# A hybrid decoder step on one core: projection steps and attention units put into one interleaved list, and the input norm done in small parts

## The chip, the cores and the metric

The kernel runs on one core of one Trainium2 chip. The metric is device time in microseconds (us); a run's time is that of one execution. The profile is one further execution, recorded by the hardware.

## The reference, cut to what matters

One layer of a decoder: an RMS norm, one input projection `w_in` to queries, keys, values and a pooling input u, stick-breaking attention (8 heads of 64) beside a multi-scale pooling mixer, an output projection, and a gated FFN with a short convolution. There are 2048 prompt rows of width 1024 behind 16 meta rows, and 8 decode rows with a paged cache. All is fp32.

```python
def rmsnorm(x, g):
    xf = x.astype(jnp.float32)
    r = lax.rsqrt(jnp.mean(xf * xf, axis=-1, keepdims=True) + EPS)
    return (xf * r * g.astype(jnp.float32)).astype(x.dtype)

h = rmsnorm(xp, norm_mix_g)
q, k, v, u = project_mix(h, w_in)
...
z = jnp.einsum('bqhd,bkhd->bhqk', q, k) * ATTN_SCALE + sb_bias[None, :, None, None]
valid = k_pos[None, :] < q_pos[:, None]
neg = jnp.where(valid, -jax.nn.softplus(z), 0.0)
suffix = lax.cumsum(neg, axis=3, reverse=True) - neg
a = jnp.where(valid, jnp.exp(jax.nn.log_sigmoid(z) + suffix), 0.0)
o = jnp.einsum('bhqk,bkhd->bqhd', a, v)
...
xp = xp + jnp.concatenate([o_attn, o_pool], axis=-1) @ w_out
```

## The kernel before

Every large product is made from fp32 numbers split in a rounded high part and a rest (`split`, L152: ScalarE copies, VectorE subtracts), in three matmuls a term (`mm3`, L156). A scheduler orders the instructions of each engine ahead of time: the order in which the program is written is a priority, an instruction takes its place when its simulated inputs and its buffer are ready, and each engine, the SP queue of the DMAs among them, then runs its own list strictly in order.

The mixer works on four *groups* of 128 projected columns (q, k, v and u of one pair of heads) and four *chunks* of 512 prompt rows. `prep_chunk` (L200) makes one chunk ready: for each of four tiles of 128 rows it loads x, squares it on ScalarE with a row sum (`rstd_of`, L130), runs twelve tiny VectorE operations for the reciprocal root (L138 to L149) and multiplies by root and norm weight (`norm_rows`, L192, with the weight broadcast over all partitions in `gmix`). Then, for each of eight blocks of 128 features, TensorE transposes the four tiles into one PSUM tile `tpx` (L209), it is split into `hk`, and `hk` is also stored to `hs_s` in DRAM (L212), from where groups 1 to 3 load it again (`load_h`, L215). `prep_small` (L222) does the same for the 24 decode and meta rows.

`group_steps(g)` (L351) lists 16 steps, four chunks by q, k, v, u. A step loads and splits weights where a group needs new ones (`load_w`, L231, for q and k together, then for v and u, with the few rows in `few_rows`, L240), and calls `project` (L303): 24 matmuls of 512 columns into `psm`, a copy to SBUF, and stores to DRAM scratch (`q_s`, `k_s`) and to the outputs, keys and values through four more transposes (`put_tok`, L294). The step of u makes window sums, and the one of chunk 1 also folds the pooling weights into the output weights (`fold_pool`, L334: two loads `wt` and a matmul on each, L346). There are 11 buffers for `hk`, so in groups 1 to 3 the last step of a chunk loads three blocks of the next chunk ahead and the other five behind its own matmuls.

`attention(hp)` (L383) works on one pair of heads in 45 *units*: a block of 128 queries (or the 16 meta rows, `bi` = -1) by a chunk of up to 512 keys, the chunks from the last key to the first. `chain` (L430) makes the scores into `z` (L450), two sigmoids on ScalarE (L451, L452), a running product on VectorE (the scan, L458) and a product that VectorE and GpSimd take in turn (L463). `weigh` (L472) follows three units later (`LAG`): it transposes the weights into `tt` (L493), copies them to SBUF on ScalarE or VectorE (L486) and multiplies by V into `po` (L508). Queries and keys come back from DRAM scratch and are split (`load_q` L387, `load_k` L399) when the first unit of a query block asks for them.

The order around the change is written out as: all 16 steps of group 0, then `attention(0)` with the steps of group 1 spread evenly between its units, `attention(1)` with group 2, `attention(2)` with group 3, then the output weights, then `attention(3)`, in which each finished block of 128 rows is followed, one block later, by its output projection and second norm (`out_tile`, L573). Decode attention and the FFN come after that, from 1175 us on.

Of the kernel before, what the change touches and what calls it, by code (L numbers as in the profile page):

```python
# [18 lines left out]
P = 128  # L19
D = 1024  # L20
# [19 lines left out]
LAG = 3  # L40
BEB, OMB, ATB = 5, 3, 4
# [17 lines left out]
def hymba_kernel(  # L59
# [70 lines left out]
    def rstd_of(pool, xt, n, sq=None):  # L130
# [6 lines left out]
        ms = pool.tile([P, 1], F32, name="ms")  # L137
        nc.vector.tensor_scalar(out=ms[:n, :], in0=ss[:n, :], scalar1=1.0 / D, scalar2=EPS, op0=ALU.mult, op1=ALU.add)  # L138
        r = pool.tile([P, 1], F32, name="rr")
        t = pool.tile([P, 1], F32, name="rt")  # L140
# [4 lines left out]
        for _ in range(3):  # L145
            nc.vector.scalar_tensor_tensor(out=t[:n, :], in0=r[:n, :], scalar=r[:n, 0:1], in1=ms[:n, :],
                                           op0=ALU.mult, op1=ALU.mult)
# [34 lines left out]
    gmix = [pb.tile([P, CW], F32, name=f"gmix{q}", tag="raw", bufs=RWB) for q in range(2)]  # L182

    def load_x(i):
        xt = pb.tile([P, 2, CW + 1], F32, name="xt", tag="om", bufs=OMB).rearrange("p a n -> p (a n)")[:, 0:D]
        x_rows(xt, i)
        if i == 1:
            for q in range(2):
                nc.sync.dma_start(out=gmix[q], in_=norm_mix_g[q * CW:(q + 1) * CW].partition_broadcast(P))
        return xt  # L190

    def norm_rows(xt, n, r):  # L192
        xn = pb.tile([P, 2, CW], F32, name="xn", tag="be", bufs=BEB).rearrange("p a n -> p (a n)")
        for q in range(2):
            cs = slice(q * CW, (q + 1) * CW)
            nc.vector.scalar_tensor_tensor(out=xn[:n, cs], in0=xt[:n, cs], scalar=r, in1=gmix[q][:n, :],
                                           op0=ALU.mult, op1=ALU.mult)
        return xn

    def prep_chunk(ch):  # L200
        xns = []
        for a in range(4):
            xt = load_x(1 + 4 * ch + a)
            xns.append(norm_rows(xt, P, rstd_of(pb, xt, P, sq=("at", ATB))[:, 0:1]))
        hk = []
        for c in range(NK):
            tp = tt_tile("tpx")
            for a in range(4):
                nc.tensor.transpose(tp[:, a, :], xns[a][:, c * P:(c + 1) * P], ident)  # L209
            hk.append(pa.tile([P, 2, CW], F32R, name="hk", bufs=HKB))  # L210
            split(hk[c][:, 0, :], hk[c][:, 1, :], tp.rearrange("p a n -> p (a n)"))
            nc.sync.dma_start(out=hs_s[ch][c], in_=f32(hk[c]))  # L212
        return hk
# [872 lines left out]
```

## Time and profile before

| what | us |
|---|---|
| median of 3 runs | 2874.93 |
| lowest and highest | 2872.41, 2880.97 |
| the profiled execution's own time | 2876.12 |
| its span, first to last instruction | 2874.3 |

In the profile, PE is TensorE's matmuls, PEld its weight loads, which overlap them, DVE is VectorE, ACT ScalarE, POOL GpSimd, SP the queue that issues nearly all DMAs. L12 is line 12 of the kernel before. Matmuls are pipelined, so busy TensorE can be TensorE that waits for its operands between two of them; what it does in a stretch is better read from how many matmuls it finishes there. PEclk is the mean clock granted to TensorE, 1.00 being 2.4 GHz; its lower level is 1.2 GHz. The view of waits and the idle time in brackets name the instruction that ended the wait last.

### The profile page before, as it was taken

The numbers are of one execution on the slowest core, as the hardware profiler recorded it, in microseconds if no ns is written. First come the engines' busy times: TensorE is split into PE (matmuls) and PEld (weight loads), VectorE is DVE, ScalarE is ACT, GpSimd is POOL, SyncE is SP. The second block draws the span as 40 slices with busy tenths as digits, with TensorE's granted clock in tenths as the row PEclk, the third lists the DMA queues.
The fourth block names the chain that finished last, engine by engine and source line by source line (L and its number), as shares of the span: only waits on it lengthen the run. The fifth ranks groups of instructions, "written<-read, shape, count | busy, mean of one in ns | idle before, by whom it ended". The sixth has DMA issues, their size and how long they took to land.

```text
span 2874.3 us, 39685 instructions
## 1 busy us (share of the span) xinstructions
PE 2724.3 (95%) x14622; PEld 2106.8 (73%) x14622; DVE 1826.1 (64%) x3101; ACT 1041.3 (36%) x1801; POOL 825.5 (29%) x995
## 2 busy tenths in 40 slices
PE   5899999999998999799999998999999999999998
PEld 4677777777776777577777776777777767777766
DVE  6556787687787778579876766677764451124433
ACT  3345665665665356322322222222222230012111
POOL 0023243333233222044554454445543200000000
PEclk9899999999998999889999999999999999999999
DMA  6674344333425332466566465546655385656552
GB/s 210 241 256 147 112 132 169 114 119 119 143 67 173 113 100 91 154 201 205 195 246 216 169 232 198 179 158 227 212 183 198 129 279 172 189 181 209 161 202 88
DMA packets 319223, 495.10 MB, mean 172 GB/s; under 512 B 24111, under 2 KB 227127, under 8 KB 302629
## 3 DMA queue, kind: packets, MB, share of 16 engines
q1 hardware_dynamic: 300597, 358.35, 38.4%
q0 software_dynamic: 18432, 134.23, 12.8%
q8 instruction: 115, 1.88, 0.3%
q14 instruction: 79, 0.65, 0.1%
HBM read 391.27 MB, written 101.64 MB: 171 GB/s over the span
## 4 chain that ended last, share of the span: by engine, by line
PE 60%; DVE 8%; DMA 4%; issue 3%; ACT 1%; POOL 0%; SPq 0%; ACTq 0%; DVEq 0%; POOLq 0%
PE psu L159 10%; PE psu L160 9%; PE psu L161 9%; PE psd L159 5%; PE psd L161 5%; PE psd L160 5%; PE dav L804 2%; PE po L508 2%; DVE kvd L736 1%; PE z L450 1%; PE pso L161 1%; PE pso L159 1%; PE pso L160 1%; PE tt L493 1%; DVE om L458 1%
## 5 line engine op out<-in xcount | busy, mean ns | idle before, releaser
L159 PE MATMUL psu<-h2c,uwh 128*128 128x512 f32 x1408 | 557.1, 396 | 0.7 <-ACT h2c L153 0.7
L160 PE MATMUL psu<-h2c,uwh 128*128 128x512 f32 x1408 | 553.2, 393 | 0.0
L161 PE MATMUL psu<-h2c,uwl 128*128 128x512 f32 x1408 | 552.9, 393 | 0.0
L458 DVE TENSOR_TENSOR_SCAN om<-om,zero 128x513 f32<-128x513 f32 (+5 forms) x360 | 381.5, 1066 | 103.4 <-ACT om L451 60.3
L884 DVE SCALAR_TENSOR_TENSOR cv<-psu,par,cv 128x511 f32<-128x511 f32 (+1 forms) x352 | 261.2, 742 | 130.3 <-ACT cv L881 129.3
L463 POOL TENSOR_TENSOR be<-be,om 128x512 f32<-128x512 f32 (+3 forms) x176 | 182.4, 1036 | 550.0 <-DVE om L458 310.5
L159 PEld LDWEIGHTS psu<-h2c,uwh 128*128 128x128 f32 x1408 | 266.5, 189 | 82.8 <-issue 15.8
L160 PEld LDWEIGHTS psu<-h2c,uwh 128*128 128x128 f32 x1408 | 266.4, 189 | 63.7 <-issue 9.7
L161 PEld LDWEIGHTS psu<-h2c,uwl 128*128 128x128 f32 x1408 | 266.2, 189 | 63.6 <-issue 8.3
L451 ACT ACTIVATE om<-z,nbias 128x512 f32<-128x512 f32 (+5 forms) x360 | 213.2, 594 | 214.0 <-PE z L450 125.4
L895 POOL TENSOR_TENSOR cv<-cv,cv 128x512 f32<-128x512 f32 x88 | 195.4, 2221 | 267.6 <-DVE cv L889 215.9
L1053 DVE TENSOR_TENSOR xt<-psd,xt 128x512 f32<-128x512 f32 x64 | 44.1, 690 | 293.6 <-PE psd L161 287.1
L881 ACT ACTIVATE cv<-psu,par 128x512 f32<-128x512 f32 x176 | 136.4, 776 | 252.1 <-PE psu L161 241.2
L154 DVE TENSOR_TENSOR uwl<-uwr,uwh 128x1024 fp32r<-128x1024 f32 x94 | 128.1, 1364 | 152.5 <-ACT uwh L153 150.2
L159 PE MATMUL psm<-hk,wh 128*128 128x512 f32 x512 | 207.2, 410 | 6.3 <-ACT wh L153 4.2
L452 ACT ACTIVATE be<-z,bias 128x512 f32<-128x512 f32 (+5 forms) x360 | 211.1, 589 | 1.0 <-PE tpx L209 0.9
L160 PE MATMUL psm<-hk,wh 128*128 128x512 f32 x512 | 209.0, 408 | 0.0
L161 PE MATMUL psm<-hk,wl 128*128 128x512 f32 x512 | 206.4, 403 | 0.0
L161 PE MATMUL psd<-wd,al 128*128 128x512 f32 x512 | 200.9, 393 | 0.0
L159 PE MATMUL psd<-wd,ah 128*128 128x512 f32 x512 | 200.8, 396 | 0.0
L160 PE MATMUL psd<-wd,ah 128*128 128x512 f32 x512 | 200.4, 392 | 0.0
L153 ACT CAST uwh<-uwr 128x1024 fp32r<-128x1024 f32 x94 | 99.0, 1056 | 270.3 <-PE psu L160 258.2
(226 smaller groups left out, 4892.1 us busy)
## 6 DMA issues: line engine op xcount, KB each, us to landing
hk<-hs_s SPq DMA_DIRECT2D x96, 512.0 KB
uwr<-in_w_up_dram SPq DMA_DIRECT2D x88, 512.0 KB
act_s<-sg SPq DMA_DIRECT2D x88, 256.0 KB
ar<-act_s SPq DMA_DIRECT2D x32, 704.0 KB
raw<-in_w_up_dram SPq DMA_DIRECT2D x40, 512.0 KB
xt<-in_x_prompt_dram SPq DMA_DIRECT2D x32, 512.0 KB
hs_s<-hk SPq DMA_DIRECT2D x32, 512.0 KB
uwr<-in_w_down_dram SPq DMA_DIRECT2D x22, 512.0 KB
```

The source lines that it names most:

```text
L153: nc.scalar.copy(hi, src)
L154: nc.vector.tensor_tensor(out=lo, in0=src, in1=f32(hi), op=ALU.subtract)
L159: nc.tensor.matmul(ps, ah, bh, start=i == 0, stop=False)
L160: nc.tensor.matmul(ps, ah, bl, start=False, stop=False)
L161: nc.tensor.matmul(ps, al, bh, start=False, stop=i == n - 1)
L451: nc.scalar.activation(out=om[:M, e, 0:n], in_=z[:M, :n], func=AF.Sigmoid, scale=-SCALE, bias=nbias[:M, h:h + 1])
L452: nc.scalar.activation(out=be[:M, e, 0:n], in_=z[:M, :n], func=AF.Sigmoid, scale=SCALE, bias=bias[:M, h:h + 1])
L458: nc.vector.tensor_tensor_scan(out=rv, data0=rv, data1=zero[:M, 0:1].broadcast_to([M, n + 1]), initial=1.0 if top else st["prev"][:M, e, 0 ...
L463: (nc.gpsimd if cnt["mul"] % 2 == 0 else nc.vector).tensor_tensor(out=be[:M, e, m0:n], in0=be[:M, e, m0:n], in1=om[:M, e, m0 + 1:n + 1], o ...
L881: nc.scalar.activation(out=t, in_=ps, func=AF.Identity, scale=cpar(2, fi), bias=cpar(3, fi))
L884: nc.vector.scalar_tensor_tensor(out=t[:, o:], in0=ps[:, 0:CW - o], scalar=cpar(d, fi), in1=t[:, o:], op0=ALU.mult, op1=ALU.add)
L895: nc.gpsimd.tensor_tensor(out=cv[1], in0=cv[0], in1=cv[1], op=ALU.mult)
```

## The change

Two things change. *The order.* The steps of all four groups stand in one list of 80 entries (`in_steps`, with the norm of chunks 1 to 3 as entries of their own, and `with_params`), followed by eight entries that load one block of the output weights each. The 180 units of the four pairs stand in another. Before unit `ui` the list is run up to the larger of two marks: an even pace that reaches the last step at unit 135, where the last pair begins, and a ramp for each of the next 24 units that reaches the step of v of the chunk that the unit needs two units (`PF`) ahead of it. `fetch` loads K, V and q of the next unit ahead of the chain of this one. Units of two pairs follow each other without a break in the pipeline of `LAG` units. The last step of a group loads the first chunk of the next group ahead.

*The norm.* Rows are scaled by the reciprocal root alone, in place; the norm weight is turned once into a column `gcol`, one value per partition, and applied where the transposed block is split (the copy on ScalarE takes it as a scale, VectorE's subtract becomes multiply and subtract). The root is computed for four tiles at once. Chunk 0 is done in one go (`prep_first`); for the others the sums of squares are taken first (`prep_squares`), and x is loaded a second time in four pieces of 256 features (`prep_piece`), each with its own scaling, transposes and splits.

```diff
+    def rstd_from(pool, ss, n):
...
+            if w == 1:
...
+            else:
+                nc.vector.tensor_tensor(out=t[:n, :], in0=r[:n, :], in1=r[:n, :], op=ALU.mult)
+                nc.vector.tensor_tensor(out=t[:n, :], in0=t[:n, :], in1=ms[:n, :], op=ALU.mult)
...
+    def turned(ch, c, part):
+        tp = tt_tile("tpx")
         for a in range(4):
+            nc.tensor.transpose(tp[:, a, :], part(a), ident)
+        tp = tp.rearrange("p a n -> p (a n)")
+        hk = pa.tile([P, 2, CW], F32R, name="hk", bufs=HKB)
+        nc.scalar.activation(out=hk[:, 0, :], in_=tp, func=AF.Copy, scale=gcol[:, c:c + 1])
+        nc.vector.scalar_tensor_tensor(out=hk[:, 1, :], in0=tp, scalar=gcol[:, c:c + 1], in1=f32(hk[:, 0, :]),
+                                       op0=ALU.mult, op1=ALU.subtract)
+        nc.sync.dma_start(out=hs_s[ch][c], in_=f32(hk))
+        hks[ch].append(hk)
+    def times_r(ap, r):
+        nc.vector.tensor_scalar(out=ap, in0=ap, scalar1=r, scalar2=None, op0=ALU.mult)
+    def prep_first():
+        ss = pb.tile([P, 4], F32, name="ss4")
+        xts = [load_x(1 + a, "be", BEB) for a in range(4)]
+        gains()
+        for a in range(4):
+            squares(xts[a], P, ss[:, a:a + 1])
+        r = rstd_from(pb, ss, P)
+        for a in range(4):
+            times_r(xts[a], r[:, a:a + 1])
...
+    def prep_squares(ch):
+        ss = pb.tile([P, 4], F32, name="ss4")
+        for a in range(4):
+            squares(load_x(1 + 4 * ch + a, "om", OMB), P, ss[:, a:a + 1])
+        rs[ch] = rstd_from(pb, ss, P)
+    def prep_piece(ch, q):
+        W = 2 * P
+        xp = pb.tile([P, 4, W], F32, name="xp", tag="be", bufs=BEB)
+        nc.sync.dma_start(out=xp, in_=x_prompt[CW * ch:CW * (ch + 1), W * q:W * (q + 1)].rearrange("(a p) d -> p a d", p=P))
+        for a in range(4):
+            times_r(xp[:, a, :], rs[ch][:, a:a + 1])
...
+        for c in range(2):
+            turned(ch, 2 * q + c, lambda a: xp[:, a, c * P:(c + 1) * P])
...
-            ahead = g and ki == 3 and ch < NCH - 1
+        nxt = (ch + 1) % NCH
+        ahead = ki == 3 and (g < 3 if ch == NCH - 1 else g > 0)
...
+    def in_steps():
+        for g in range(4):
+            for ch in range(NCH):
+                for ki in range(4):
+                    if g == 0 and ch < NCH - 1 and ki == 3:
+                        yield lambda ch=ch: prep_piece(ch + 1, 0), None
+                    yield lambda g=g, ch=ch, ki=ki: step(g, ch, ki), ((g, ch) if ki == 2 else None)
+                    if g == 0 and ch < NCH - 1:
+                        if ki == 0:
+                            yield lambda ch=ch: prep_squares(ch + 1), None
+                        if ki == 3:
+                            for q in range(1, 4):
+                                yield lambda ch=ch, q=q: prep_piece(ch + 1, q), None
...
-    for hp in range(3):
-        attention(hp, group_steps(hp + 1), lambda bi: None)
-    inp.close()
...
+    prep_first()
+    prep_small()
...
+    needs = [ready[ui // per, min((un[0] + 1) // 4, 3)] for ui, (_, un) in enumerate(units)]
+    first = needs[0]
+    END = 3 * per
...
+    for ui, (h, un) in enumerate(units):
+        want = max(first + (n - first) * (ui + 1) // max(u - PF, 1) if u - PF > ui else n
+                   for u, n in enumerate(needs[:ui + 24]))
+        fill_to(max(want if ui else first, min(n_in, first + (n_in - first) * ui // END)))
+        if ui == 0:
+            h[1](*un)
+        if ui + 1 < len(units):
+            units[ui + 1][0][1](*units[ui + 1][1])
+        pend.append((h, h[2](*un), un))
+        if len(pend) > LAG:
+            h_, ab, un_ = pend.pop(0)
+            h_[3](ab, *un_)
+        if ui + 1 >= END:
+            if at_ < len(fill):
+                fill_to(at_ + 2)
+            elif len(finished) > 1:
+                out_tile(finished.pop(0))
```

Here `h[1]` is `fetch`, `h[2]` `chain` and `h[3]` `weigh` of the unit's pair; `step` has the body of the steps before, without the norm.

## Rows read from the trace of the kernel before

**Rows 1.** The page: span, and part 1, busy us, share of the span, instructions.
```profile
span 2874.3 us, 39685 instructions
...
PE 2724.3 (95%) x14622; PEld 2106.8 (73%) x14622; DVE 1826.1 (64%) x3101; ACT 1041.3 (36%) x1801; POOL 825.5 (29%) x995
```

**Rows 2.** Windows, all engines: length; PE, PEld, DVE, ACT, POOL busy (count); PEclk; DMA share; GB/s.
```profile
0.00:200.00 200.00, 152.89 (x767) 120.56 (x768) 112.08 (x360) 82.44 (x158) 18.69 (x81) 0.91 0.71 239
200.00:400.00 200.00, 197.79 (x1371) 155.80 (x1371) 143.63 (x207) 122.15 (x243) 59.22 (x116) 1.00 0.39 132
400.00:475.00 75.00, 66.02 (x467) 50.54 (x463) 60.66 (x111) 46.06 (x105) 34.10 (x68) 0.95 0.50 155
...
625.00:700.00 75.00, 67.38 (x452) 50.45 (x451) 61.77 (x111) 47.71 (x109) 35.10 (x70) 0.91 0.46 145
```

**Rows 3.** Windows, all engines, three stretches of 25 us.
```profile
25.00:50.00 25.00, 19.07 (x111) 14.71 (x111) 21.14 (x84) 10.68 (x20) 0.00 (x0) 0.90 0.93 322
100.00:125.00 25.00, 14.31 (x53) 9.68 (x51) 11.63 (x36) 9.00 (x17) 0.00 (x0) 0.66 0.58 183
1275.00:1300.00 25.00, 25.00 (x112) 20.71 (x111) 24.93 (x27) 7.92 (x10) 15.11 (x8) 1.00 0.59 200
```

**Rows 4.** Windows, TensorE's instructions on `psm` (projections): busy (count), PEclk, DMA, GB/s.
```profile
0.00:200.00 200.00, 118.64 (x447) 0.91 0.71 239
200.00:400.00 200.00, 97.48 (x371) 1.00 0.39 132
400.00:475.00 75.00, 24.37 (x92) 0.95 0.50 155
475.00:625.00 150.00, 76.93 (x292) 1.00 0.37 126
625.00:700.00 75.00, 23.65 (x82) 0.91 0.46 145
700.00:825.00 125.00, 64.15 (x240) 1.00 0.28 98
825.00:860.00 35.00, 3.91 (x16) 1.00 0.26 80
```

**Rows 5.** Windows, TensorE's instructions on `po` (attention times V).
```profile
0.00:200.00 200.00, 0.39 (x2) 0.91 0.71 239
200.00:400.00 200.00, 41.26 (x518) 1.00 0.39 132
400.00:475.00 75.00, 14.06 (x160) 0.95 0.50 155
475.00:625.00 150.00, 30.61 (x400) 1.00 0.37 126
625.00:700.00 75.00, 14.15 (x153) 0.91 0.46 145
700.00:825.00 125.00, 25.68 (x334) 1.00 0.28 98
825.00:860.00 35.00, 9.59 (x128) 1.00 0.26 80
```

**Rows 6.** Timeline, TensorE: start, us, instruction, count, idle before and its releaser.
```profile
25.20 1.22 PE L159 MATMUL psm<-hk,wh 128*128 128x512 f32 x2 [0.25 <-ACT hk L153]
...
111.20 2.05 PE L346 MATMUL pkw<-wt,pT 128*128 128x512 f32 x2 [7.39 <-DMA wt<-in_w_out_dram]
...
858.29 0.17 PE L450 MATMUL z<-kst,qh 128*16 128x16 f32 x1
```

**Rows 7.** Groups by shape, 0 to 1250 us: count, busy us, mean ns, idle before.
```profile
L209 PE MATMUL tpx<-ident,xn 128*128 128x128 f32 x128 | 24.4, 330 | 23.6 <-DVE xn L196 21.4 <-ACT wf L348 2.2
...
L146 DVE SCALAR_TENSOR_TENSOR rt<-rr,ms 128x1 f32<-128x1 f32 x96 | 23.1, 243 | 2.0
L196 DVE SCALAR_TENSOR_TENSOR xn<-xt,rr,gmix 128x512 f32<-128x512 f32 x32 | 22.4, 748 | 0.7 <-PE tpx L209 0.6
```

**Rows 8.** DMA issues, 0 to 200 us: count, KB each.
```profile
hk<-hs_s SPq DMA_DIRECT2D x11, 512.0 KB
```

More of the change, by code (lines that the diff above doesn't have):

```diff
@@ new lines, in squares, with gains @@
+    def squares(xt, n, ss):
+        sq = pb.tile([P, D], BF16, name="sq", tag="at", bufs=ATB)
+        nc.scalar.activation(out=sq[:n, :], in_=xt[:n, :], func=AF.Square, accum_out=ss)
+    def gains():
+        gr = pb.tile([P, P], F32, name="gr", tag="ot")
+        nc.sync.dma_start(out=gr[:NK, :], in_=norm_mix_g.rearrange("(c p) -> c p", p=P))
+        tp = tt_tile("tpg")
+        nc.tensor.transpose(tp[:, 0, 0:NK], gr[:NK, :], ident[:NK, :NK])
+        nc.vector.tensor_copy(gcol, tp[:, 0, 0:NK])
@@ L381, in key_lo, with attention @@
         return 0 if j == 0 else META + P * (j - 1)
-    def attention(hp, fill, done):
+    def attention(hp):
         kst, vts, qs_, st, vtm = {}, {}, {}, {}, []
@@ L428, in attention, with fetch @@
                 units.append((bi, c, c == ctop, c == 0))
+        def fetch(bi, c, top, low):
+            for c_ in range(c + 1):
+                if (c_, 0) not in kst:
+                    load_k(c_)
+            g = bi // 4 if bi >= 0 else -1
+            if (g, 0) not in qs_:
+                load_q(g)
         def chain(bi, c, top, low):
@@ L517, in weigh @@
                 nc.sync.dma_start(out=cat_s[hp, :, NS + q0:NS + q0 + M], in_=ot[:, :M])
-                done(bi)
-        pend, at_ = [], 0
-        for ui, un in enumerate(units):
-            pend.append((chain(*un), un))
-            if len(pend) > LAG:
-                weigh(pend[0][0], *pend.pop(0)[1])
-            while at_ < len(fill) * (ui + 1) // len(units):
-                fill[at_]()
-                at_ += 1
-        for be, un in pend:
-            weigh(be, *un)
+                if hp == 3 and bi >= 0:
+                    finished.append(bi)
+        return units, fetch, chain, weigh
     def with_params():
@@ L593, in out_tile, with fill_to @@
         nc.sync.dma_start(out=h2_s[c0:c0 + n, :], in_=xn)
-    late = []
-    def out_later(bi):
-        late.append(bi)
-        if len(late) > 1:
-            out_tile(late.pop(0))
-    attention(3, [], out_later)
-    out_tile(late.pop())
+    prep_first()
+    prep_small()
+    fill, ready = [], {}
+    for fn, key in in_steps():
+        fill.append(fn)
+        if key:
+            ready[key] = len(fill)
+        if len(fill) == 1:
+            fill.append(with_params)
+    n_in = len(fill)
+    fill += [lambda c=c: load_out(c) for c in range(NK)]
+    heads = [attention(hp) for hp in range(4)]
+    units = [(h, un) for h in heads for un in h[0]]
+    per = len(heads[0][0])
+    needs = [ready[ui // per, min((un[0] + 1) // 4, 3)] for ui, (_, un) in enumerate(units)]
+    first = needs[0]
+    END = 3 * per
+    at_, pend = 0, []
+    def fill_to(n):
+        nonlocal at_
+        while at_ < min(n, len(fill)):
+            fill[at_]()
+            at_ += 1
+    for ui, (h, un) in enumerate(units):
[15 more added lines that the diff above has]
+                out_tile(finished.pop(0))
+    for h_, ab, un_ in pend:
+        h_[3](ab, *un_)
+    for bi in finished:
+        out_tile(bi)
     main.close()
```

131 lines of the change are left out of this document (53 added, 78 removed).

## The prediction

> **What bounds the kernel now.** I read the page's engine totals first: TensorE is busy for 95% of the span and VectorE for 64% [rows 1], so only stretches in which TensorE is held up can give time. Then the busy time by stretch up to 860 us, where the chains of the last head pair begin [rows 2, 6]; everything behind that (out tiles, FFN, 2014 us) keeps its code and its place, and I leave it alone. Busy time hides how densely TensorE is fed, so I counted work: the projections' matmuls and the matmuls into `po`, by the same stretches [rows 4, 5]. Where 512-column matmuls follow each other without a gap, 112 fit into 25 us, 0.223 us each [rows 3]. In the three stretches where projections and attention run side by side (200 to 400, 475 to 625, 700 to 825, clock 1.00 in the one shown) 903 projection matmuls take 201 us by that price; the other 274 of 475 us belong to 1252 `po` matmuls: 0.22 us each, with all that goes with them (scores, transposes of weights, token copies). These two prices are the filled rate.
>
> At it the first 860 us hold 1540 x 0.223 = 343 us of projections, 1695 x 0.22 = 373 us of attention and 24 us of norm transposes [rows 4, 5, 7]: 740 us. So 120 us are lost, and the rows say where. 0 to 200: 447 x 0.223 + 24 = 124 of 200 us, 76 lost, of which 25 pass before the first projection matmul [rows 4, 6, 7]. 400 to 475: 92 x 0.223 + 160 x 0.22 = 56, 19 lost; 625 to 700: 18 + 34 = 52, 23 lost: the changes from one head pair to the next, where projections run out. 825 to 860: 4 + 28 = 32, 3 lost. The sum, 121, agrees.
>
> **The change part by part.** *Norm of chunk 0.* All four x tiles now have buffers at once; four squares, one Newton run of 15 small operations instead of four of 12, four scalings of 1024 columns, then the transposes. The costliest small kind takes 0.24 us [rows 7], so at most 3.6 us instead of 11.5, which were partly interleaved. A scaling has no row; the nearest is the two-tensor product it replaces, 0.748 us for 512 columns [rows 7], so at most 1.5 us each, and at least the 0.24 us of a tiny operation. I take the upper end, being the same engine on the same data: 6 us. From the last tile (some 12 us, an estimate from four loads that need no buffer) through square, Newton, scaling and first split, the first matmul comes at about 23 us instead of 25.2; bounds 20 and 27.
>
> The Trainium skill, VectorE: DVE Perf Modes, section Mode 2x_2P, says that a one-tensor fp32 operation within SBUF yields two elements a cycle and a two-tensor one only one. By it the four scalings take 3 us, and the total is 3 us lower, 2835. No row of before has such an operation of that width.
>
> *Norm of chunks 1 to 3.* Off the path of the end, but on VectorE: 24 two-tensor products of 512 columns go, 48 scalings of 256 come (by 0.374 us, 18 us for 18 us), and about 100 small operations go: up to 24 us less work in a stretch where VectorE is busy 112 of 200 us [rows 2, 7]. The gain multiplied into the split costs nothing: ScalarE copies 512 columns anyway, and VectorE's subtract becomes a three-operand pass of the same length. If VectorE were full there, 32 such passes would add a few us at most. The SP queue gets 12 loads of 512 KB more (x is read twice) and loses two broadcasts: 6.3 MB, at the 322 GB/s of 25 to 50 us [rows 3] 20 us of transfer. The 0 to 200 stretch moves 239 GB/s [rows 2]; with these and the same time it would be 271, still below that, so I cost it at nothing; without this cover it is 20 us. Queued behind a piece's load on SP are the stores of projected keys and the loads of K, V and q; the units wait for those.
>
> *Group 0 interleaved with head pair 0.* From the list rule I worked out where each entry falls (180 units, 45 a pair; 80 entries). Chunk 0 is projected to v ahead of unit 0, chunk 1 ahead of unit 1, chunk 2 ahead of unit 9, chunk 3 ahead of unit 21; they are needed at units 0, 4, 12 and 24. The 51 us lost between 25 and 200 us are holes that attention of pair 0 can now fill, since its units no longer come behind all 16 steps. One of them is plain: TensorE, in order, stands 7.39 us for the `fold_pool` weights at 111 us [rows 6], and the 25 us around it have 14.31 us busy at a clock of 0.66 [rows 3]. That step stays in order and can stand again. Bounds for what stays of the 51: 10 (this hole) and 51; I take half, 25, because at the filled rate VectorE is already busy 144 of 200 us [rows 2] and here it has the norm on top.
>
> *Head pair changes.* The steps of the next group no longer stop and start with a pair; a unit's K, V and q are fetched one unit early. But the small units and the splits of K and q, which fill VectorE there (61 and 62 of 75 us [rows 2]), stay. Bounds 0 and 42 us left; I take the middle, 21. Loading the next group's chunk 0 from the last step of the group before is worth nothing: 11 such loads already happen within the first 200 us [rows 8], ahead of need.
>
> *Stretches without steps.* The rule puts no step at units 10 to 15, 22 to 36 and 67 to 77. There the tail of pair 2 is the nearest row: 128 `po` matmuls and 16 of projections in 35 us [rows 4, 5], 0.245 us a `po`. For 32 units of some 16 `po` matmuls that is 0.025 x 510 = 13 us; bounds 0 (later steps are run early) and twice that. I take 10.
>
> *Output weights.* Eight loads and splits move to four units from unit 134 on; the last projection stays at unit 135, so they start when they did: nothing. Out tiles keep their lag of one.
>
> **Sum.** Lost after: 23 + 25 + 21 + 3 + 10 = 82 us against 120: 38 us less. The profiled execution took 2876.1 us (span 2874.3), 1.2 us over the median of the runs; 2876 - 38 = 2838 us, and I give that for the median too.
>
> **The rivals.** *A, every hole fills.* Only the start, the fold hole and the 3 us stay: 23 + 10 + 3 = 36, so 84 us go: 2792 us. For it: TensorE is busy 197.8 of 200 us where both kinds of work are at hand [rows 2]. Against: VectorE is at 81 and 82% in the very holes [rows 2].
>
> *B, the holes move.* Instructions are already issued when a planner thinks them ready (group 1's chunk loads within group 0's stretch [rows 8]), so the new list may alter little: 40 of 51 stay at the start, 35 of 42 at the changes, 15 in the empty stretches: 23 + 40 + 35 + 3 + 15 = 116, 4 us less: 2872 us. It includes the case that the change of order hardly takes effect.
>
> *C, slower: units wait for a chunk just projected.* Units 0, 4, 12 and 24 each need keys that a few units before were still being projected, stored to DRAM and loaded again, through the one SP queue behind x pieces and 512 KB stores. Before, only one such edge shows, at 100 to 125 us: 10.7 us idle, and 14.3 us at 0.66 of the clock lose another 4.9 [rows 3]: 15.6 us. Four of them on top of the forecast are 62 us: 2900 us. It decides from 12 us an edge on (38 + 9 over four). For it: the planner did not foresee the 7.39 us wait. Against: TensorE has prep and u steps to run meanwhile. The Trainium skill, TensorE: Matmul & The Clock Gate, Part 1, says that the slow clock is the default and activity releases it; the trace agrees, 0.66 around a 7.39 us wait. By that such an edge costs more than its idle time, as priced.
>
> **How the numbers follow.** Forecast 0.50, A 0.13, B 0.20, C 0.17. A measurement of this kernel can tell about 0.3%, 9 us, from no change. The forecast and A are faster, and a quarter of B (holes closing a little more): 0.68; the rest of B 0.15; C 0.17 slower. Range 2795 to 2886: from just over A to the near half of C, with the bounds of the start, the first stretch and the changes of pair inside.
>
> **What would show it.** Right: a projection matmul before 24 us; `po` matmuls in dozens before 150 us; the 16-column scores of the last pair near 820 us instead of 858; stretches around the pair changes at over 75% of the filled rate; the span from there to the end still near 2014 us. Wrong: granted clock below 0.9 over several windows between 50 and 250 us, or waits of `z` on K and q splits by the dozen (C); the last pair beginning near 855 us with VectorE over 90% busy for long stretches (B); or a longer end, which I hold unchanged.

## The result, and the profile after

The changed kernel takes 2837.3 us (median of 4 runs, 2836.4 to 2838.1), the kernel before 2876.7 us in the same runs: a ratio of 0.9863, with a 95% interval of 0.9846 to 0.9880. The prediction was 2838 us, range 2795 to 2886. The number is right. Its terms are not all right: one of them is missing in the chip's time, and two that were put at nothing are there instead.

The page of the profiled execution (2838.1 us), span and TensorE's total, answers to [rows 1].

```profile
span 2836.4 us, 39537 instructions
...
PE 2708.9 (96%) x14623; PEld 2093.9 (74%) x14623; DVE 1806.2 (64%) x2989; ACT 1039.8 (37%) x1801; POOL 816.5 (29%) x995
```

TensorE does the same work (one record more), and the span is 37.9 us shorter, so the time came out of its idle stretches and of its clock. To see which, the span is cut by the work rather than by the time: a stretch of 70 us at each change of head pair (from 5 us ahead of the 16-column scores of the new pair), 80 us around the end of the projections (from 30 us ahead of the last pair's first score), and what lies between. Windows, all engines, of the changed kernel; columns as in [rows 2]:

```profile
0.00:25.00 25.00, 6.11 (x22) 4.64 (x23) 11.69 (x45) 16.00 (x26) 3.00 (x43) 1.00 0.78 251
25.00:100.00 75.00, 61.80 (x337) 50.25 (x337) 35.92 (x104) 30.47 (x59) 8.71 (x25) 0.89 0.73 245
100.00:200.00 100.00, 86.39 (x517) 63.40 (x516) 75.36 (x142) 58.73 (x123) 27.68 (x58) 0.95 0.51 171
200.00:331.40 131.40, 124.71 (x902) 95.96 (x902) 103.94 (x149) 86.79 (x170) 38.40 (x73) 1.00 0.46 154
331.40:401.40 70.00, 68.77 (x425) 53.56 (x426) 40.00 (x73) 35.37 (x82) 22.58 (x53) 1.00 0.57 191
401.40:563.80 162.40, 156.58 (x1141) 122.41 (x1141) 134.32 (x183) 107.42 (x215) 58.94 (x104) 0.99 0.34 110
563.80:633.80 70.00, 70.00 (x436) 55.62 (x435) 48.34 (x81) 38.72 (x87) 23.98 (x58) 1.00 0.59 204
633.80:807.30 173.50, 172.21 (x1175) 137.20 (x1176) 121.52 (x177) 99.21 (x199) 46.31 (x89) 1.00 0.45 149
807.30:887.30 80.00, 74.00 (x517) 57.30 (x511) 68.97 (x108) 58.73 (x122) 33.92 (x68) 0.94 0.47 139
```

The same view of the kernel before, at the stretches that answer to these (its pairs change at 401.3, 633.0 and 858.3 us):

```profile
0.00:25.00 25.00, 3.58 (x12) 2.01 (x12) 15.21 (x72) 10.92 (x17) 2.91 (x42) 1.00 0.60 189
25.00:100.00 75.00, 62.91 (x327) 50.19 (x328) 46.70 (x180) 29.24 (x54) 0.00 (x0) 0.89 0.73 253
100.00:200.00 100.00, 86.41 (x430) 68.37 (x429) 50.16 (x112) 42.28 (x88) 15.78 (x39) 0.91 0.71 242
200.00:396.30 196.30, 194.25 (x1345) 153.13 (x1343) 140.04 (x203) 118.68 (x236) 59.22 (x116) 1.00 0.40 133
396.30:466.30 70.00, 60.86 (x425) 45.85 (x424) 57.71 (x106) 45.47 (x104) 32.97 (x66) 0.95 0.55 168
466.30:628.00 161.70, 160.67 (x1115) 127.48 (x1114) 118.13 (x157) 99.73 (x196) 48.57 (x91) 1.00 0.35 119
628.00:698.00 70.00, 62.38 (x410) 46.93 (x410) 58.44 (x107) 44.02 (x101) 34.31 (x68) 0.90 0.48 151
698.00:828.30 130.30, 129.77 (x907) 102.79 (x906) 94.60 (x127) 78.92 (x156) 37.61 (x76) 1.00 0.27 95
828.30:908.30 80.00, 65.26 (x428) 49.74 (x427) 72.70 (x106) 55.91 (x114) 34.04 (x60) 0.87 0.50 149
```

Two things in such a row are loss: the length less TensorE's busy time, and the share of the clock that was not granted, times the length. At the first change of pair before, that is 70 - 60.86 = 9.1 us idle and 0.05 x 70 = 3.5 us of clock, 12.6 us; after, 1.2 us and nothing. In this way, all in us:

| stretch | before | after |
|---|---|---|
| 0 to 25 us | 21.4 | 18.9 |
| 25 to 200 us | 42.9 | 40.1 |
| 200 us to the first change of pair | 2.1 | 6.7 |
| first change of pair (70 us) | 12.6 | 1.2 |
| between | 1.0 | 7.4 |
| second change of pair (70 us) | 14.6 | 0.0 |
| between | 0.5 | 1.3 |
| end of the projections (80 us) | 25.1 | 10.8 |
| sum | 120.2 | 86.4 |

So the two changes of pair gave 26 us, the end of the projections 14 us, the start 2.5 us, and the first stretch only 3 us; 12 us went back in the stretches in between, where the list has no steps for long. That is 34 us. By milestones it is 21.0 us at the last pair's first score and 28.4 us at the first matmul of the FFN part (1231.5 before, 1203.1 after). The table is too high, since it takes the clock's share of the whole length, idle time included: with the trace's clock records laid over TensorE's busy time alone, the sums are 111.3 and 82.3 us, 29 us less, and the first stretch has 0.4 us less instead of 3. Another 9.5 us are missing in the FFN part itself (1642.8 to 1633.3 us), of which no line was changed.

### The profile page after: what moved, and what is told of

Read it like the earlier page. It is cut to its first block, busy times and chain, and to the rows that moved or that the text cites. A ratio compares the mean times of both kernels' runs of the same rounds, so it can differ in the third digit from the quotient of the medians.

```text
span 2836.4 us, 39537 instructions
## 1 busy us (share of the span) xinstructions
PE 2708.9 (96%) x14623; PEld 2093.9 (74%) x14623; DVE 1806.2 (64%) x2989; ACT 1039.8 (37%) x1801; POOL 816.5 (29%) x995
## 4 chain that ended last, share of the span: by engine, by line
PE 76%; DVE 11%; DMA 5%; issue 4%; ACT 2%; POOL 1%; SPq 0%; DVEq 0%; POOLq 0%; ACTq 0%
PE psu L169 10%; PE psu L170 10%; PE psu L171 10%; PE psd L169 5%; PE psd L171 5%; PE psd L170 5%; PE po L567 4%; PE psm L169 4%; PE psm L170 4%; PE psm L171 3%; DVE om L517 3%; PE z L509 3%; PE tt L552 3%; PE dav L886 2%; PE pso L169 1%
## 5 line engine op out<-in xcount | busy, mean ns | idle before, releaser
L522 POOL TENSOR_TENSOR be<-be,om 128x512 f32<-128x512 f32 (+3 forms) x176 | 188.1, 1069 | 554.7 <-DVE om L517 354.7
L966 DVE SCALAR_TENSOR_TENSOR cv<-psu,par,cv 128x511 f32<-128x511 f32 x352 | 260.8, 742 | 129.4 <-ACT cv L963 128.4
L169 PEld LDWEIGHTS psu<-h2c,uwh 128*128 128x128 f32 x1408 | 265.2, 188 | 79.7 <-issue 14.1
```

The source lines that it names most:

```text
L169: nc.tensor.matmul(ps, ah, bh, start=i == 0, stop=False)
L522: (nc.gpsimd if cnt["mul"] % 2 == 0 else nc.vector).tensor_tensor(out=be[:M, e, m0:n], in0=be[:M, e, m0:n], in1=om[:M, e, m0 + 1:n + 1], o ...
L966: nc.vector.scalar_tensor_tensor(out=t[:, o:], in0=ps[:, 0:CW - o], scalar=cpar(d, fi), in1=t[:, o:], op0=ALU.mult, op1=ALU.add)
```

## The experiments

Each run is compared with the kernel before, run on the same chip (medians 2875.5 to 2877.3 us). "First FFN matmul" is the start of the first `psu` matmul in the run's timeline: 1231.5 us before, 1203.1 after.

### The norm alone

The kernel before, with the new norm and nothing else; steps and units in the old order.

```diff
-            xt = load_x(1 + 4 * ch + a)
-            xns.append(norm_rows(xt, P, rstd_of(pb, xt, P, sq=("at", ATB))[:, 0:1]))
...
+                    prep_squares(ch)
+                    for q in range(4):
+                        prep_piece(ch, q)
```

> The kernel before with the new norm alone (one rstd for four tiles, pieces of 256 features, the weight in the split of the transposed rows), in the old order of steps and units. What it leaves out is the one list: the early units, the earlier fetch, the loads of hk at a group's end. Theory (the norm is worth only its part of the start, where the first projection came 3.2 us earlier in the changed kernel): 2870 to 2875 us, 3 us under the kernel before. Rival (the norm keeps VectorE from holding up the projections all through the first stretch, where 51 us were lost before): 2850 to 2858 us. Second rival (the shorter norm chain is behind the 9.5 us that the FFN part also lost): span from the first FFN matmul to the end near 1633 instead of 1643 us.

Measured 2872.9 us, ratio 0.9988 (0.9977 to 0.9999); first FFN matmul at 1233.6 us, the FFN part 1644.4 us. The theory holds: the first projection comes at 21.0 us instead of 25.2, and by the median that is what the norm is worth. Between 25 and 200 us it loses about as much as the kernel before (44.5 us, 42.9 before). The profiled execution was the slowest of its ten (2879.7 us), and in it the 4 us of the start are gone again by the first FFN matmul, 2 us later than before. One price can be read off in the changed kernel. DVE groups by shape, 0 to 250 us:

```profile
L218 DVE SCALAR_TENSOR_TENSOR hk<-tpx,gcol,hk 128x512 fp32r<-128x512 f32 x32 | 23.2, 744 | 20.5 <-ACT hk L217 20.3
...
L224 DVE TENSOR_SCALAR xt<-xt,rr 128x1024 f32<-128x1024 f32 x4 | 2.7, 750 | 0.0
```

A scaling of 1024 columns takes 750 ns, what the two-tensor product took for 512 [rows 7]. The Trainium skill, VectorE: DVE Perf Modes, section Mode 2x_2P, says that a one-tensor fp32 operation within SBUF yields two elements a cycle; the trace agrees, and the four scalings cost 3 us, not the 6 us taken.

### Group 0 ahead of the units, and where a group starts

Four kernels make a square: group 0's 32 entries ahead of unit 0, or spread over units 0 to 21 as in the change; and the first steps of groups 2 and 3 right behind a change of pair (units 48 and 93; the pairs change at 45 and 90) or between changes (units 63 and 100). All four keep the new norm and the one list. Each is the changed kernel with one line replaced. Group 0 first, even pace:

```diff
-        fill_to(max(want if ui else first, min(n_in, first + (n_in - first) * ui // END)))
+        fill_to(32 + (n_in - 32) * ui // END if ui < END else n_in)
```

> The changed kernel with all 32 entries of group 0 ahead of unit 0, and the other 48 spread evenly over units 0 to 135: the early units and the empty stretches are undone, while the norm, the fetch one unit ahead across pairs and the loads of hk at a group's end stay. Theory (the early units gained nothing, as the losses of 50 us before and after in the first stretch say, and the empty stretches cost 11 us that now go): 2825 to 2840 us. Rival (as predicted: early units fill 25 us of the first stretch's holes): 2855 to 2865 us. Both expect the pair changes to cost about 17 us for the first two, as in the changed kernel.

Measured 2872.6 us, ratio 0.9983 (0.9974 to 0.9993). Both expectations fell: with the old pace nearly the whole gain is gone, changes of pair included. So neither the one list nor the fetch across a change of pair closes those holes; the places of the steps do.

Group 0 interleaved, even pace for the rest:

```diff
+        even = 32 + (n_in - 32) * (ui - 22) // (END - 22) if ui >= 22 else first
+        fill_to(max(want if ui else first, min(n_in, even)))
```

> The changed kernel with group 0 between units 0 to 21 as it is, but the other 48 entries spread evenly over units 22 to 135, so that no stretch of units is without steps. Theory (the stretches without steps, units 22 to 36 and 67 to 77, lose about 11 us that an even pace fills): 2825 to 2831 us. Rival (what is lost there only moves: the steps taken from the later stretches leave as much idle there): 2835 to 2840 us. Second rival (the steps of a group come too late for the next pair's first units): above 2842 us, with the 16-column scores of pairs 1 to 3 later than 336, 569 and 837 us.

Measured 2840.3 us, ratio 0.9870 (0.9853 to 0.9886). The rival, just above its range: what is lost in the stretches without steps only moves. By the same reckoning, the two stretches ahead of the second change of pair in which the changed kernel has the long gaps lose 3.5 us instead of 14.1, and what follows, from the second change to the end of the projections, 24.2 instead of 12.1. Its first FFN matmul comes at 1202.7 us, as in the changed kernel.

Group 0 first, but the groups' starts moved between the changes:

```diff
+        pts = [(0, 32), (60, 48), (97, 64), (135, 80)]
+        even = next((x + (y - x) * (ui - a) // (b - a) for (a, x), (b, y) in zip(pts, pts[1:]) if a <= ui < b), n_in)
+        fill_to(even)
```

> As the run with group 0 ahead of unit 0 (2872.6 us), but with the other 48 entries paced so that the first step of group 2 falls on unit 63 and of group 3 on unit 100, as with the even pace after group 0, instead of on units 48 and 93, next to the changes of pair at units 45 and 90. The first change of pair is met with one step every 3.75 units (2.8 in the run it is made from), the second with one every 2.3. Theory (the losses around 400 to 450 and 650 to 700 us come from the loads, splits and few rows of a new group that fall together with a change of pair): 2840 to 2848 us, both losses gone. Rival A (it is how dense the steps are around the change): the first loss stays or grows, the second shrinks; 2855 to 2865 us. Rival B (it is the early units that removed the losses): 2868 to 2876 us.

Measured 2857.3 us, ratio 0.9935 (0.9916 to 0.9955): half of the gain, by the numbers that rival A gave.

Group 0 interleaved, but the groups' starts at the changes (the same lines with these points, and group 0 as in the change):

```diff
+        pts = [(22, 32), (45, 48), (90, 64), (135, 80)]
```

> As the run with an even pace after group 0 (2840.3 us), group 0 between units 0 to 21 as in the changed kernel, but with the other 48 entries paced so that the first steps of groups 2 and 3 fall on units 48 and 93, right behind the changes of pair at units 45 and 90. Nothing else moves. Theory (a new group that starts at a change of pair costs 15 to 20 us each): 2865 to 2878 us. Rival (early units are what counts, the place of a group's start does not): 2838 to 2845 us.

Measured 2871.0 us, ratio 0.9976 (0.9964 to 0.9989), as the theory said: the places of 48 steps take back 31 us, with group 0 interleaved all the same. Windows, all engines, at the first and second change of pair and the end of the projections. Group 0 first, even pace (2872.6 us):

```profile
396.70:466.70 70.00, 61.47 (x415) 46.28 (x415) 57.27 (x105) 44.62 (x103) 32.83 (x66) 0.93 0.54 166
629.40:699.40 70.00, 60.95 (x405) 45.79 (x405) 58.16 (x107) 44.17 (x101) 34.68 (x68) 0.90 0.49 149
831.60:911.60 80.00, 66.95 (x448) 50.88 (x447) 73.58 (x108) 56.09 (x116) 35.38 (x62) 0.81 0.51 148
```

Group 0 interleaved, starts at the changes (2871.0 us):

```profile
385.50:455.50 70.00, 65.88 (x444) 51.31 (x444) 50.46 (x94) 38.93 (x91) 24.06 (x58) 0.98 0.70 223
621.10:691.10 70.00, 60.20 (x413) 45.26 (x413) 58.48 (x107) 43.93 (x101) 32.78 (x66) 0.95 0.50 153
820.70:900.70 80.00, 63.96 (x414) 48.40 (x413) 71.31 (x104) 54.05 (x112) 33.58 (x60) 0.83 0.50 147
```

Group 0 first, starts between (2857.3 us):

```profile
383.40:453.40 70.00, 60.13 (x449) 45.68 (x447) 59.41 (x100) 47.61 (x112) 33.35 (x75) 0.95 0.27 83
606.20:676.20 70.00, 69.12 (x488) 54.44 (x487) 55.82 (x95) 44.03 (x103) 26.01 (x64) 1.00 0.56 176
813.90:893.90 80.00, 71.62 (x466) 55.71 (x464) 71.67 (x105) 55.56 (x113) 33.62 (x63) 0.85 0.51 147
```

Group 0 interleaved, starts between (2840.3 us):

```profile
353.90:423.90 70.00, 70.00 (x469) 55.57 (x468) 52.20 (x90) 43.01 (x98) 24.26 (x61) 1.00 0.57 189
...
593.60:663.60 70.00, 67.29 (x477) 52.45 (x476) 53.16 (x91) 43.22 (x102) 28.52 (x65) 1.00 0.50 152
...
803.20:883.20 80.00, 73.13 (x493) 55.39 (x492) 71.64 (x108) 58.88 (x122) 35.90 (x66) 0.89 0.46 135
```

Read as above, idle and clock together, with the steps per unit of the list at that change (worked out from the edits) and the time by which the last projection lies ahead of the last pair's first score:

| kernel | first change | second change | end of projections | last projection ahead by |
|---|---|---|---|---|
| group 0 first, starts at changes | 13.4 us at 0.36 | 16.1 us at 0.36 | 28.3 us | 26 us |
| interleaved, starts at changes | 5.5 us, 0.70 then 0.36 | 13.3 us at 0.36 | 29.6 us | 26 us |
| group 0 first, starts between | 13.4 us at 0.27 | 0.9 us at 0.43 | 20.4 us | 11 us |
| interleaved, starts between | 0.0 us at 0.42 | 2.7 us at 0.42 | 15.7 us | 7 us |

The profiled executions of the two interleaved kernels took 5 and 6 us more than their medians. The changed kernel itself, by its own rule, runs 12 entries over the 20 units around each of the two changes (0.6 a unit), starts groups 2 and 3 at units 80 and 108, and loses 1.2, 0.0 and 10.8 us, with the last projection 0.2 us ahead.

Two things meet at a change of pair. One is how many steps there are to fill it: without a group's start, 0.27 steps a unit leave 13.4 us open and 0.42 nearly nothing. The other is the group's start: at 0.36 with a start 13 to 16 us are lost, while the joined version below, at 0.37 without one, loses 3.2 us (with group 0 interleaved). What each of the two is worth alone the square does not show: at the second change the start and the pace move together, and at the first the place of group 0 moves too. The third column is read as a matter of supply, which the next run tries: the thinner the pace, the earlier TensorE's stream runs out of projections.

### The projections' end

The changed kernel, with the last 14 entries paced to end five units earlier.

```diff
+        even = first + (n_in - first) * ui // END if ui < 111 else 66 + (n_in - 66) * (ui - 111) // 19
+        fill_to(max(want if ui else first, min(n_in, even)))
```

> The changed kernel (2837.3 us), with the last 14 entries of the projections paced to end at unit 130 instead of 135, denser from unit 111 on. The last projection then lies some 25 us ahead of the last pair's first score, as it did in the kernel before (831.8 against 858.3 us). Theory (from 30 us ahead of the last pair to 50 us behind its start, PE's idle time and the clock's share fell from 24.9 to 11.1 us only because projections now last until the pair begins): 2845 to 2851 us, the time of the first FFN matmul 8 to 14 us later than 1203.1 us. Rival (it is the load of the output weights, which falls in the same place in both): 2835 to 2840 us.

Measured 2850.9 us, ratio 0.9912 (0.9895 to 0.9928), first FFN matmul at 1212.4 us, 9.3 us later. The theory holds. The last projection starts at 821.9 us, 20 us ahead of the last pair's first score at 842.0; the window around it:

```profile
812.00:892.00 80.00, 68.63 (x417) 53.42 (x416) 66.34 (x99) 52.42 (x108) 31.67 (x56) 0.81 0.50 147
```

11.4 us idle and 15.2 us of clock, 26.6 us against 10.8 in the changed kernel, with the output weights loaded at the same place of the list. It is the projections that were missing, as in the kernel before. In the changed kernel they last up to the pair's first score; timeline, TensorE:

```profile
837.09 0.39 PE L171 MATMUL psm<-hk,wl 128*128 128x512 f32 x1
837.31 0.17 PE L509 MATMUL z<-kst,qh 128*16 128x16 f32 x1
```

### The fetch one unit ahead

```diff
-        if ui == 0:
+        if un[2]:
             h[1](*un)
-        if ui + 1 < len(units):
-            units[ui + 1][0][1](*units[ui + 1][1])
```

> The changed kernel, but K, V and q of a block are fetched when the block's own first unit starts its chain, not one unit ahead. Theory (the first two changes of pair lost 42 us before and 17 after, and the fetch one unit ahead is what made the difference): 2852 to 2865 us, with PE waiting on the loads and their splits at 336, 569 and 837 us. Rival (the prediction's zero: the projection steps that now run through the changes of pair are the cover, and the loads are early enough): 2835 to 2840 us.

Measured 2835.6 us, ratio 0.9861 (0.9844 to 0.9877): the rival, and for a plain reason. On every engine, and in SP's list of transfers, the two programs hold the same instructions in the same order: the order is planned when the program is built, and it had placed these loads by itself. So what loads that really come later would cost is not tried. The run is a repeat of the changed kernel, and shows how far two profiles of one program differ: its first FFN matmul comes at 1199.7 us instead of 1203.1, with 1.2 and 0.0 us lost at the two changes in both.

### The first stretch

The loss between 25 and 200 us (51 us by the prediction's prices, 43 by the table) stayed. TensorE's two longest waits there, in the timeline of the changed kernel, and the windows behind the second:

```profile
45.69 0.45 PE L590 MATMUL pkp<-ident,ra 128*128 128x128 f32 x1 [5.09 <-DMA ra<-in_conv_w_dram]
...
71.45 1.12 PE L345 MATMUL pk<-ident,kf 128*128 128x128 f32 x4 [6.26 <-ACT kf L376]
```

```profile
62.00:72.00 10.00, 3.50 (x40) 2.79 (x35) 7.90 (x35) 3.23 (x8) 2.88 (x9) 0.73 0.84 258
72.00:82.00 10.00, 10.00 (x50) 8.88 (x49) 7.15 (x12) 7.24 (x13) 3.60 (x8) 0.75 0.78 284
```

A hole of 6 us is followed by 10 us at 0.75 of the clock. The copy that ended it came late itself; timeline, ScalarE:

```profile
70.81 0.59 ACT L376 COPY kf<-psm 128x512 f32<-128x512 f32 x1 [5.09 <-DVE sb L336]
```

ScalarE stood 5.1 us for a small operation of VectorE, and VectorE's timeline has all 16 scalings of the next chunk (`xp`, the new norm's pieces) ahead of that operation, with two waits of 1 us for their loads among them. So the change's own early norm is in this chain. Two edits aim at such waits. The parameters ahead of the norm:

```diff
+    with_params()
     prep_first()
...
-            fill.append(with_params)
+            fill.append(lambda: None)
```

> The changed kernel, with the small parameters (their loads, two transposes of them, four of the pool state) ahead of the first norm, instead of behind the first projection step. Theory (the waits of 5.1 us for the loads and 6.3 us behind them, with the lower granted clock that follows each, between 42 and 82 us, go): 2827 to 2833 us. Rival (the first stretch is held by its loads, and the wait moves ahead of the first projection): 2835 to 2841 us.

Measured 2838.2 us, ratio 0.9869 (0.9851 to 0.9887). Both of these waits are gone from the list, but others of 4.1 us (`tpx` on `xp`), 3.5 us (`tpx` on `hk`) and 2.3 us (`wr`) stand there instead, and 37.6 us are lost between 25 and 200 us against 40.1 (36 in the repeat of the changed kernel): the rival. The stretch is not quite untouched by the early units: the three kernels with the new norm and group 0 first lose 44 to 47 us here, so against them it is some 4 to 11 us less.

Group 0's fold two chunks later:

```diff
-        if (ch, ki) == (1, 3):
+        if (ch, ki) == ((3, 1) if g == 0 else (1, 3)):
```

> The changed kernel, with fold_pool of group 0 at chunk 3 (behind k) instead of chunk 1 (behind u). Theory (each hole of the first stretch is a wait that PE's written order did not foresee, so early units cannot fill it; this one, 4.4 us of waits on pl, wt and pT near 119 us with the granted clock at 0.69 behind it, goes only if its loads come early): first FFN matmul 3 to 6 us earlier than 1203.1 us; as PE's written order has 801 FFN matmuls ahead of the first dav here, 6 to 9 us are lost there again, so the whole stays at 2836 to 2843 us. Rival (the hole is filled by nothing else and moves with the fold): first FFN matmul at 1202 to 1205 us and 2842 to 2847 us in all.

Measured 2853.3 us, ratio 0.9916 (0.9898 to 0.9935), first FFN matmul at 1218.5 us. Both expectations fell; it is 16 us slower. Timeline of TensorE, then windows:

```profile
233.61 2.04 PE L394 MATMUL pkw<-wt,pT 128*128 128x512 f32 x2 [12.41 <-DMA wt<-in_w_out_dram]
```

```profile
225.00:235.00 10.00, 1.39 (x2) 0.50 (x2) 0.66 (x3) 0.50 (x2) 0.00 (x0) 0.50 0.72 270
235.00:245.00 10.00, 8.78 (x41) 6.91 (x42) 2.50 (x5) 4.12 (x8) 0.98 (x2) 0.67 0.34 111
```

SP's queue issues the load of this `wt` behind eight loads of `hk` of 512 KB, 4.7 us after TensorE began to wait:

```profile
217.44 3.22 SPq L264 DMA_DIRECT2D hk<-hs_s  x5
...
222.09 2.88 SPq L264 DMA_DIRECT2D hk<-hs_s  x3
225.89 0.33 SPq L392 DMA_DIRECT2D wt<-in_w_out_dram  x1
```

(That it would land earlier ahead of them was not tried.) TensorE is in the midst of attention of pair 0, with scores and products of several units in its stream, and still nothing fills the 12.4 us: they stand behind the waiting matmul. So this hole is not a lack of work but one late transfer at a fixed place of the stream. That the holes of the first stretch are of this kind is argued from it, from the two waits above, and from the waits that came up when those two went; each of them was not tried. The clock is at 0.50, its lower level of 1.2 GHz, in the first of these windows. The Trainium skill, TensorE: Matmul & The Clock Gate, Part 1, says that activity releases the slow clock; here it was at 0.67 in the ten us behind the wait and at 1.00 in the next ten, and the trace agrees.

### The FFN part

No line of it was changed, and it took 9.5 us less. PE's waits from the end of the out tiles to 1520 us show a wait of the first value product of the decode step in the kernel before, and none in the changed one:

```profile
PE dav L804 <- DVE zdec L738: 3.6, 1, 3.6
```

In the built program 801 FFN matmuls stand ahead of the first `dav` before, and 815 after: the planned order fell out otherwise. An edit of the kernel before puts the values two places later:

```diff
-            order += [("w", b)] + [t for x in range(16) for t in (8 * b + 16 + x, 64 + 8 * b + x)]
+            ks, vs = list(range(8 * b + 16, 8 * b + 32)), list(range(64 + 8 * b, 80 + 8 * b))
+            order += [("w", b)] + ks[:2] + [t for x in range(14) for t in (vs[x], ks[x + 2])] + vs[14:]
```

> The kernel before, with one edit in the FFN part that the change does not touch: in the list of the decode steps, each run of 16 keys and 16 values has the values two places later, so that PE's written order has 821 FFN matmuls ahead of the first value product (dav) where the kernel before has 801 and the changed kernel 815. Theory (the FFN part of the changed kernel took 9.5 us less because the written order fell out so that dav no longer waits for VectorE's zdec, 3.6 us, with 3.4 us lost to the clock behind it): 2867 to 2871 us, no wait of dav, the FFN part near 1633 us instead of 1643. Rival (the 9.5 us come from the state in which the changed kernel reaches the FFN part, not from the place of dav): 2874 to 2879 us.

Measured 2874.9 us, ratio 0.9996 (0.9986 to 1.0005). Its profile has the wait gone (same view):

```profile
PE dav L804 <- issue: 0.5, 1, 0.5
```

and an FFN part of 1636.7 us, 6.1 us less than before; yet the median is that of the kernel before, in the rival's range. Over the profiles, the FFN part is 1633.0 to 1637.6 us with 815 matmuls ahead of `dav` (three kernels, two of them the same program), 1635.9 to 1644.4 with 801 (eight) and 1636.7 to 1639.4 with 821 (three): as a whole, the sizes overlap. At `dav` they do not. From the 800th to the 900th FFN matmul it is 28.2 us with 815 ahead, 29.0 with 821, and 30.5 to 34.7 with 801. The kernel before has 34.7 there and the changed one 28.2, which is 6.5 of the 9.5 us. Windows, all engines, from 5 us ahead of the first `dav`, before, then after:

```profile
1422.90:1462.90 40.00, 36.41 (x165) 25.95 (x164) 28.57 (x39) 9.23 (x12) 22.04 (x16) 0.91 0.86 306
```

```profile
1395.60:1435.60 40.00, 40.00 (x196) 28.97 (x195) 29.12 (x35) 8.91 (x12) 24.87 (x18) 1.00 0.82 297
```

Before, 3.6 us idle and 3.6 us of clock; after, nothing. So the planned order sets these 6.5 us, and the other 3 us stay open. So does the median of the run with the values later: its profile wins 5.7 us at this place and has 4.9 us more ahead of the FFN part, where TensorE's order is that of the kernel before.

### Joined versions

Parameters first, values later, and a pace by pieces with no stretch without steps and no start at a change:

```diff
+        pts = [(22, 32), (65, 48), (104, 64), (135, 80)]
```

> A version meant to beat both: the changed kernel with the parameters first, the entries of groups 1 to 3 paced by pieces (32 at unit 22, 48 at 65, 64 at 104, 80 at 135: no stretch without steps, no group's start at a change of pair, densest ahead of the last pair), and the decode values two places later. Theory (the three parts add: 4 us of the first stretch, 4 to 8 us of the stretches without steps, and no wait of dav): 2823 to 2832 us. Rival (they share one cover, and what is filled at one place is missing at another): 2833 to 2840 us.

Measured 2841.8 us, ratio 0.9876 (0.9860 to 0.9893): worse than either expectation. Windows at its first change of pair, and between the changes:

```profile
350.20:420.20 70.00, 68.16 (x438) 53.43 (x437) 51.18 (x87) 43.61 (x100) 27.03 (x60) 0.98 0.42 139
420.20:589.40 169.20, 164.97 (x1158) 129.50 (x1156) 122.46 (x177) 104.22 (x208) 50.82 (x100) 0.98 0.42 139
```

The first row is the 1.8 us idle and 1.4 us of clock used above. The second has no stretch without steps, but a group's start, and loses 4.2 + 3.4 us: as much as the empty stretch of the changed kernel.

> The changed kernel with the parameters first (that alone: 2838.2 us, first FFN matmul at 1199.0 us, a wait of dav of 2.2 us) and the decode values two places later (alone, on the kernel before: no wait of dav, the FFN part 6.1 us shorter in its profile, the whole unchanged). Theory (the 4 us won ahead of the FFN part are real and were given back at dav): 2830 to 2834 us. Rival (both are within what one instruction stream varies from run to run): 2835 to 2840 us.

Measured 2838.9 us, ratio 0.9872 (0.9856 to 0.9889): the rival. No version beat the changed kernel; what differs among the last of them is within what one program varies.

## Why the prediction was right, and where not

**The start.** Predicted at 23 us instead of 25.2; the first projection came at 22.0. The 2.5 us less in the table agree.

**The first stretch (predicted 25 us less of 51).** This is the step that failed. The table has 3 us, and the repeat of the changed kernel 7 us. At the prediction's own prices the first 200 us of the changed kernel hold 316 x 0.223 + 162 x 0.22 = 106 us and 23 us of norm transposes; of the 71 us left, 22 pass ahead of the first projection, so 49 of the 51 us stayed. The reasoning, "holes that attention of pair 0 can now fill", took a hole for a lack of work. The units did come early (36 `po` matmuls between 100 and 150 us, the first at 104 us instead of 194), but the two longest holes are waits at fixed places, and the run with the fold moved shows a wait of 12.4 us in the midst of ready attention that nothing fills. What the prediction said of one hole, that it "stays in order and can stand again", holds for these too.

**Head pair changes (predicted 21 of 42 us less).** By the table 26 of 27 us are gone. The count of work agrees as well. Windows of the changed kernel at both changes, TensorE on `psm`, then on `po`, as in [rows 4, 5]:

```profile
331.40:401.40 70.00, 41.33 (x164) 1.00 0.57 191
563.80:633.80 70.00, 44.67 (x175) 1.00 0.59 204
```

```profile
331.40:401.40 70.00, 11.51 (x130) 1.00 0.57 191
563.80:633.80 70.00, 11.41 (x130) 1.00 0.59 204
```

At the prediction's prices that is 164 x 0.223 + 130 x 0.22 = 65 of 70 us, or 93% of the filled rate, and 97% at the second; over 75% was looked for. The cause was half named. That the steps "no longer stop and start with a pair" is it; the fetch one unit early, named beside it, adds nothing as it is written, as the program is the same without it, and does not suffice, as the kernel with group 0 first has it too. The square of four runs says what the step left out: one list does next to nothing by itself (2872.6 us), and where the groups' starts and the dense part of the list fall decides.

**Stretches without steps (predicted 10 us).** The table has 11.8 us more in the three rows between. The size was right; but they are not a cost that an even pace saves (2840.3 us): it closes these gaps and loses as much at the second change and behind it, where the steps held back were the filler. In the gaps VectorE is nearly full. A window of the changed kernel in the longest one, from 463 to 514 us, in which no projection matmul starts; VectorE is busy for 9.56 of 10 us:

```profile
481.40:491.40 10.00, 8.69 (x79) 6.26 (x80) 9.56 (x12) 7.52 (x17) 5.46 (x10) 1.00 0.03 8
```

**The end of the projections (held at 3 us lost).** 14 us were won here, predicted at nothing. The prediction counted 3 us in 825 to 860 us at its prices and put the projections' end at unit 135 in both kernels. In the trace before, the last projection lies at 831.8 us, 26 us ahead of the pair's first score [rows 6]; after, 0.2 us ahead. The run that ends them early has the loss back: 26.6 us in that window, 13.6 us in all. It could have been read in the timeline of the kernel before.

**The rest.** From the last pair's first score to the end "near 2014 us" was 2016.0 before and is 1999.1: 7.4 us less to the first FFN matmul and 9.5 in the FFN part, 6.5 of them at the first value product of the decode step. The prediction held this span because its code was unchanged; the planned order of its instructions was not. The score itself was looked for near 820 us and came at 837.3, which is 21 us earlier rather than 38.

**The rivals.** A and C did not come: among TensorE's waits of the first 340 us none is of `z` on a split of K or q, as C had it. C's other sign, the clock below 0.9, did come: 0.83, 0.65, 0.66 and 0.83 in four windows of 10 us between 60 and 150 us. The kernel before has five such windows between 50 and 130 us (0.74, 0.66, 0.82, 0.50, 0.82), so that sign told nothing. B, in which the list hardly takes effect, is what the kernel with group 0 first and the old pace is: 2872.6 us where B gave 2872.

So the sum agreed because a term that was at least 22 us too large stood against 14 us and 9.5 us that were not in it, with 5 us more at the changes than taken and other small ones. The sign and the place of the largest gain, the changes of pair, were argued rightly; the agreement to one us is luck.

## What to carry to other kernels

Before counting a hole as room for other work, look at what ended it: if it is one late transfer at a fixed place of an in-order stream, work that is ready does not help; what moving that instruction or its load does has to be tried, since here one such move cost 16 us and another gained nothing. Where filler is scarce, the question is where it lies: hold it back for the stretches of short units, keep a new group's loads and splits away from them, and let it last until the stage ends. A total that agrees proves no term of it; compare the stages, cut by the work and not by the clock on the wall.

## What was not expected

- Removing the fetch one unit ahead left every engine's instructions the same, in the same order.
- The kernel before and the one with the values later share TensorE's order up to the FFN part, and still took 373.2 and 378.3 us from the last pair's first score to the first FFN matmul: differences of 5 us between two profiles say nothing by themselves.
- Moving one small step by two chunks cost 16 us: 12.4 us of one wait, and in the 20 us around it the granted clock at 0.50 and 0.67.
